# Down projection by block products: residual tiles made by GpSimd in the places of the first token sums, and added behind the sixth and the seventh product

## The chip, the core and the metric

The kernel runs on one core of a Trainium2 chip. The metric is the device time of one execution in microseconds; lower is better. The core has five engines that work side by side, each through its own queue in order: PE (TensorE, matmuls), DVE (VectorE), ACT (ScalarE), POOL (GpSimd) and SP (SyncE, which here only issues DMAs). Semaphores hold an instruction until what it needs is there, and whatever stands behind it on its engine waits as well.

## The reference, cut to what matters

One layer of an encoder with 1024 tokens of width 1024: a token mixer, cross-attention and a gated ConvFFN, each followed by a LayerNorm over the scaled input plus the result. The change lies in the last of them:

```python
h = layer_norm(DN_ALPHA * h + conv_ffn(h, w_up, b_up, w_dw, b_dw, w_down, b_down), ln3_w, ln3_b)
# conv_ffn ends in
y = jax.nn.gelu(g, approximate=False) * u        # 1024 tokens x 2816
return y @ w_down + b_down                       # 2816 x 1024
```

So the output is LayerNorm(y @ w_down + r), where r = DN_ALPHA * h + b_down is called the residual here.

## The kernel before

Everything runs in fp16 pairs: a number is split into a high and a low half (`split16`, lines 203 to 205: ACT writes the high half, DVE the low half in line 205), and each product takes three matmuls (`mm3`, lines 225 to 227).

The 2816 rows of `w_down` are 22 chunks of 128. The first 16 are multiplied by blocks in a scheme with seven products instead of eight, on sums and differences of the blocks. A product (`dprod`, line 1830) is 96 matmuls of 128x512 into four banks of PSUM. `X4` names the four banks of the products 1, 4 and 6, `W4` those of 5 and 7, `Z4` those of 2 and 3. The token sums come from `a_sums` (line 1794) and lie in four tiles made by `s_home`: X1l and X2l for the products 4 and 5, Yl and X2h for 6 and 7. In the trace they are called SX1l, SX2l, SYl and SX2h. The products 4 to 7 run with `outer=True`: the eight row blocks are the outer loop, the four banks the inner one, so the fifth product is done with SX1l in its first half and with SX2l in its second.

`into` (line 1941) brings banks to the eight result tiles `C[0]` to `C[7]` (128 tokens x 1024 each; in the trace D, and for the last two junk and unitA), by DVE in line 1945 (add or subtract) or by ACT in line 1947 (copy). The sixth product goes from X4 to both halves of C[4] to C[7] (lines 2009 and 2010), the seventh from W4 to the second halves of C[0] to C[3] (line 2012).

The residual of tile `tt` is made by `rest` (line 1997): a DMA of 512 KB from `h2_d` (line 2000), times `rw` (2001), plus `rb` (2002), and then added to C[tt] (2003). The first six are made by GpSimd in the two `wraw` buffers, the last two by DVE in a raw buffer of which there are three (`raw8`: two of the name two, one of the name ur). The same three raw buffers take the loads of the y pairs (`y_pair`, line 1839) and of the weight pairs (`w_pair`, line 1847), 1 MB each, which are split for the plain product.

The plain product (lines 2019 to 2032) covers the last six chunks. Per tile, in `order` [4, 5, 6, 7, 0, 1, 2, 3], and per half of the columns, 18 matmuls go into a bank `dn`; DVE scales it and adds it to C[tt] (line 2028, the eviction). Then `ln_tile` normalizes: DVE statistics (lines 240 to 244), a small GpSimd power (245), DVE (254), ACT (255), DVE (258) and a GpSimd addition of the bias (259); the last tile takes a shorter way (251, 252). SP stores the tile. The eight banks that `dn` takes in turn are those of X4 first (four banks), then those of W4.

The order in which each engine, SP's DMA queue among them, gets its instructions isn't written out: a planner walks through a timeline of its own and, whenever an engine is free in it, takes the earliest instruction of the program that would be ready. On the chip this order stands. Where several instructions touch one tile, they keep the order of the program.

Of the kernel before, what the change touches and what calls it, by code (L numbers as in the profile page):

```python
# [8 lines left out]
F32 = mybir.dt.float32  # L9
# [5 lines left out]
OP = mybir.AluOpType  # L15
PSUM = bass.MemoryType.PSUM

D = 1024
# [7 lines left out]
WP = 1088  # L26
# [30 lines left out]
def encoder(ctx, tc, I, out):  # L57
    nc = tc.nc
    V, A, G, T, S = nc.vector, nc.scalar, nc.gpsimd, nc.tensor, nc.sync
    anchor = [None]  # L60

    def bcast_row(ap, n, off=0):
        return bass.AP(tensor=ap.tensor, offset=ap.offset + off, ap=[[0, 128], [1, n]])
# [4 lines left out]
    wp = ctx.enter_context(tc.tile_pool(name="weights", bufs=1, reuse_waits="tile"))  # L68
    xp = ctx.enter_context(tc.tile_pool(name="acts", bufs=1, reuse_waits="tile"))
# [9 lines left out]
    def bank(name):  # L79
        key = "mem" if name == "tk" else name  # L80
        turn[key] = turn.get(key, -1) + 1
        tag = SET[name][turn[key] % len(SET[name])]
        return pp.tile([128, 512], F32, name=name, tag=tag, bufs=NB[tag])
# [29 lines left out]
    def vec(i, name):  # L113
        t = vecs.tile([128, D], F32, name=f"vec{i}", tag=f"vec{i}")
        S.dma_start(t, bcast_row(I[name], D))
        return t
# [107 lines left out]
    def mm3(ps, lh, ll, rh, rl, first, last, skip=False):  # L224
        T.matmul(ps, lh, rh, start=first, stop=False, skip_group_check=skip)  # L225
        T.matmul(ps, lh, rl, start=False, stop=False, skip_group_check=skip)  # L226
        return T.matmul(ps, ll, rh, start=False, stop=last, skip_group_check=skip)  # L227
# [1049 lines left out]
    with ExitStack() as cb_:  # L1277
# [41 lines left out]
        def raw8(shape=[128, 2 * D]):  # L1319
            i = raws[0] % 3  # L1320
            raws[0] += 1
            return rt2.tile(shape, F32, name=f"two{i}") if i < 2 else pools["ur"].tile(shape, F32, name="ur")
# [16 lines left out]
        with ExitStack() as cB:  # L1339
            lw, lb = vec(0, "ln1_w"), vec(1, "ln1_b")  # L1340
# [48 lines left out]
        def to_B1(r, tt):  # L1389

            o = slice(tt // 2 * 128, tt // 2 * 128 + 128)
            pts = []
            for q in range(2):
                pt = tbank()
                for k in range(4):
                    T.transpose(pt[:, k, :], r[:, (4 * q + k) * 128:(4 * q + k + 1) * 128], ident)
                pts.append(pt)
            B1 = B1s[:, tt // 2]
            spare = lambda i: vecs.tile([128, D], F32, name=f"spare{i}", tag=f"vec{i}")
            if tt % 2:  # L1400
                if tt == todo[-1]:
                    r = spare(1)
                dst = [r[:, i * 512:i * 512 + 512].rearrange("p (k t) -> p k t", k=4) for i in range(2)]
            else:
                dst = [B1[:, q] for q in range(2)]
            for q in range(2):
                for k in range(4):
                    i = 4 * q + k
                    evict_wb(q, dst[q][:, k], pts[q][:, k], wb2, i)
            if tt % 2 == 0:  # L1410
                for q in range(2):
                    A.activation(Bh[:, 0, q, :, o], B1[:, q], AF.Copy)
                    V.tensor_tensor(Bh[:, 1, q, :, o], B1[:, q], Bh[:, 0, q, :, o], OP.subtract)
                return
            return dst
# [246 lines left out]
        tt = rq[0][1]  # L1662
        t = to_B1(*rq.pop(0))
# [27 lines left out]
        with ExitStack() as cE:  # L1691
# [36 lines left out]
            def take(v, what):  # L1728
                bg, bu, Cg, Cu = first_half(v)
                (g0, g1), (u0, u1) = ([C[:, 1:SEQ + 1].rearrange("p (j a t) -> p a j t", a=2, t=128)[:, a]  # L1730
                                       for a in range(2)] for C in (Cg, Cu))
                j4 = lambda t: t.rearrange("p (j t) -> p j t", t=128)
                c = units.s[v][1]
                if what == "m1":
                    return A.activation(g0, j4(X[v]), AF.Identity, scale=c, bias=bg)
                elif what == "C11":
                    V.scalar_tensor_tensor(g0, j4(Z[v]), c, g0, op0=OP.mult, op1=OP.add)
                elif what == "u2":
                    return A.activation(g1, j4(X[v]), AF.Identity, scale=c, bias=bg)
                elif what == "u3":  # L1740
                    A.activation(u1, j4(X[v]), AF.Identity, scale=c, bias=bu)
                elif what == "C22":
                    V.scalar_tensor_tensor(u1, j4(W[v]), c, u1, op0=OP.mult, op1=OP.add)
                elif what == "C21":
                    A.activation(u0, j4(X[v]), AF.Identity, scale=c, bias=bu)
                elif what == "C12":
                    V.scalar_tensor_tensor(g1, j4(W[v]), c, g1, op0=OP.mult, op1=OP.add)  # L1747
# [82 lines left out]
            def dprod(banks, a, b, first, js=range(4), outer=False):  # L1830
                for j, i in [(j, i) for i in range(8) for j in js] if outer else [(j, i) for j in js for i in range(8)]:
                    t = slice(j * 128, j * 128 + 128)
                    h, l = a[i]
                    mm3(banks[j], h[:, t], l[:, t], *BF_[b][i], first and i == 0, i == 7, skip=True)
# [9 lines left out]
            def w_pair(i, h, l):  # L1844

                raw = raw8()
                S.dma_start(raw, I["w_dr"][i])
                split16(h, l, raw, sd)
                for n in range(2):
                    wl[NG + 2 * i + n] = tuple(t[:, n * 1024:n * 1024 + 1024] for t in (h, l))  # L1850
# [8 lines left out]
            for v in range(NFF):  # L1859
# [6 lines left out]
                if v > 1:  # L1866
                    first = take(v, "m1")
# [12 lines left out]
                second = take(v, "u2")  # L1880
# [55 lines left out]
        with ExitStack() as cF:  # L1936
            wk = cF.enter_context(tc.tile_pool(name="wkF", bufs=1, reuse_waits="tile"))
            C = [wk.tile([128, D], F32, name=f"D{i}") for i in range(6)]
            C += [junk.bitcast(F32), kept["A"][:, :2 * D].bitcast(F32)]

            def into(banks, a, c, how):
                for j in range(4):
                    t = C[4 * a + j][:, c * 512:c * 512 + 512]
                    if how in (OP.add, OP.subtract):
                        V.tensor_tensor(t, t, banks[j], how)
                    else:
                        A.activation(t, banks[j], AF.Copy, scale=how)
# [36 lines left out]
            rw, rb, bd = vec(0, "ln2_w"), vec(1, "ln2_b"), vec(2, "b_down")  # L1984
# [9 lines left out]
            y_pair(NG + 4, sy[1][1], *(t.rearrange("p (f t) -> p f t", f=2) for t in W5))  # L1994
            order = [4, 5, 6, 7, 0, 1, 2, 3]

            def rest(n, eng, r):

                tt = order[n]
                S.dma_start(r, h2_d[tt * 128:(tt + 1) * 128, :])  # L2000
                eng.tensor_tensor(r, r, rw, OP.mult)  # L2001
                eng.tensor_tensor(r, r, rb, OP.add)
                eng.tensor_tensor(C[tt], C[tt], r, OP.add)

            for n in range(6):
                rest(n, G, wp.tile([128, WP], F32, name="wraw", tag="wraw", bufs=2)[:, :D])
            for m in range(2):
                w_pair(m, *YH[m])
            into(X4, 1, 0, OP.add)
            into(X4, 1, 1, OP.subtract)  # L2010
            dprod(W4, n4, "B22", False, outer=True)
            into(W4, 0, 1, OP.add)
            w_pair(2, *H1[0])
            two_r, lb = raw8(), raw8()[:, :D]
            S.dma_start(lb, bcast_row(I["ln3_b"], D))
            for n in range(6, 8):
                rest(n, V, two_r[:, n % 2 * D:n % 2 * D + D])

            for tt in order:
                r = C[tt]  # L2020
                last = tt == order[-1]
                for a, n in ((0, 512), (512, 256), (768, 256)) if last else ((0, 512), (512, 512)):
                    p = bank("dn")[:, :n]
# [6 lines left out]
                for i in range(2 if last else 1):  # L2030
                    c = slice(i * 512, i * 512 + 512) if last else slice(0, D)
# [90 lines left out]
```

## Time and profile before

| | us |
|---|---|
| median of 3 runs | 1458.49 (1458.29 to 1461.16) |
| the profiled execution | 1463.53 |
| its span | 1461.7 |
| PE busy | 1417.5 (97%) |
| DVE busy | 1108.8 (76%) |
| ACT busy | 852.6 (58%) |
| POOL busy | 661.3 (45%) |

The busy times are sums over the whole span, in which the engines work side by side. What an edit near the end is worth is read from that stretch alone: in rows of a window, a timeline or the waits, whose times count from the start of the span. A row of a timeline gives the start, the duration, the engine, the line, what it writes and reads, and in brackets how long the engine was idle before and what ended that. PEclk is the clock that was granted to TensorE, as a share of full speed. Rows with a count (x2) merge instructions that follow each other.

### The profile page before, as it was taken

To read this page: it belongs to the slowest core of one execution; us is meant where nothing else is said; L and a number is where in the kernel's file an instruction comes from. 1 tells how busy PE (TensorE), PEld (TensorE's weight loads), DVE (VectorE), ACT (ScalarE), POOL (GpSimd) and SP (SyncE) were. 2 spreads that over 40 slices of the span, in tenths; PEclk is the share of its full clock that TensorE was granted. 3 is DMA by queue.
4 is the path that set the end of the run, shared out by engine and by line. 5 is a ranking of instruction groups with operands and counts; after the bars stand their busy time and mean duration, and the time that the engine had idled before them with its cause. 6 is when DMAs were issued, how large, how long until landed. Compare 5 with 4: busy or idle time off the path is not lost. (4 is left out here: it accounts for less than half of the span.)

```text
span 1461.7 us, 21452 instructions
## 1 busy us (share of the span) xinstructions
PE 1417.5 (97%) x7864; PEld 834.8 (57%) x7864; DVE 1108.8 (76%) x1986; ACT 852.6 (58%) x1399; POOL 661.3 (45%) x522
## 2 busy tenths in 40 slices
PE   8999899999999999999999999999999999999797
PEld 6999777456766777674444444444444444444344
DVE  7877866635677787679657778888888878989775
ACT  5765464664554476614446667888777858645111
POOL 4452347502232866235304154487778830004943
PEclk9999999999999999999999999999999999999999
DMA  8855654324554634653442423335444357998302
GB/s 304 306 199 177 187 184 158 113 51 113 148 158 137 222 126 142 217 179 100 106 110 85 136 87 115 118 119 189 155 151 162 137 181 231 322 321 307 136 36 87
DMA packets 133298, 237.98 MB, mean 163 GB/s; under 512 B 41284, under 2 KB 84548, under 8 KB 129479
## 3 DMA queue, kind: packets, MB, share of 16 engines
q1 hardware_dynamic: 130592, 227.44, 46.9%
q0 software_dynamic: 2448, 8.88, 1.6%
q8 instruction: 62, 1.02, 0.3%
q14 instruction: 46, 0.37, 0.1%
q10 hardware_dynamic: 150, 0.27, 0.1%
HBM read 175.12 MB, written 53.54 MB: 156 GB/s over the span
## 5 line engine op out<-in xcount | busy, mean ns | idle before, releaser
L1710 DVE SCALAR_TENSOR_TENSOR cbuf<-C,wdw,cbuf 128x1024 f32<-128x1024 f32 x44 | 69.9, 1590 | 34.6 <-ACT cbuf L1709 34.6
L227 PEld LDWEIGHTS <-wlo 128*128 128x128 f16 x574 | 56.2, 98 | 61.3 <-DVE wlo L205 2.2
L225 PEld LDWEIGHTS <-whi 128*128 128x128 f16 x574 | 56.3, 98 | 60.0 <-issue 3.5
L226 PEld LDWEIGHTS <-whi 128*128 128x128 f16 x574 | 56.3, 98 | 58.4 <-issue 1.9
L2001 POOL TENSOR_TENSOR wraw<-wraw,vec 128x1024 f32<-128x1024 f32 x6 | 17.1, 2850 | 156.8 <-DMA wraw<-h 156.8
L245 POOL TENSOR_TENSOR lnrs<-lnrs,mhalf 128x1 f32<-128x1 f32 x32 | 23.4, 732 | 137.1 <-DVE lnrs L244 130.2
L1711 DVE SCALAR_TENSOR_TENSOR cbuf<-C,wdw,cbuf 128x1024 f32<-128x1024 f32 x44 | 75.6, 1721 | 1.1
L205 DVE SCALAR_TENSOR_TENSOR wlo<-wraw,us,whi 128x1024 f16<-128x1024 f32 (+1 forms) x48 | 62.1, 1314 | 18.5 <-ACT whi L204 18.5
L1709 ACT ACTIVATE cbuf<-C,bdw,wdw 128x1024 f32<-128x1024 f32 x44 | 54.4, 1238 | 19.2 <-DVE C L1747 18.5
L204 ACT ACTIVATE whi<-wraw,us 128x1024 f16<-128x1024 f32 (+1 forms) x48 | 51.0, 1103 | 15.8 <-DVE us L177 15.3
L1568 POOL TENSOR_TENSOR wraw<-two 128x512 f32<-128x512 f32 x15 | 30.5, 2031 | 64.6 <-issue 39.1
L225 PE MATMUL tk<-whi,Bo 128*128 128x256 f16 (+1 forms) x192 | 53.7, 280 | 1.6 <-DVE stage L205 1.6
L227 PE MATMUL tk<-whi,Bo 128*128 128x256 f16 (+1 forms) x192 | 53.7, 280 | 0.0
L226 PE MATMUL tk<-wlo,Bo 128*128 128x256 f16 (+1 forms) x192 | 53.7, 280 | 0.0
L226 PE MATMUL tk<-wlo,Be 128*128 128x256 f16 (+1 forms) x192 | 52.4, 274 | 0.8 <-DVE wlo L205 0.8
L225 PE MATMUL tk<-whi,Be 128*128 128x256 f16 (+1 forms) x192 | 52.6, 274 | 0.5 <-DVE stage L205 0.5
L227 PE MATMUL tk<-whi,Be 128*128 128x256 f16 (+1 forms) x192 | 52.5, 274 | 0.0
L225 PE MATMUL S<-kq,h1T 128*128 128x512 f16 x128 | 48.5, 379 | 0.0
L226 PE MATMUL S<-kq,h1T 128*128 128x512 f16 x128 | 48.5, 379 | 0.0
L227 PE MATMUL S<-kq,h1T 128*128 128x512 f16 x128 | 48.5, 379 | 0.0
L922 POOL TENSOR_SCALAR_AFFINE_SELECT whi<-whi 128x512 f32<-128x512 f32 x16 | 10.1, 634 | 82.9 <-ACT whi L919 79.6
L1238 ACT ACTIVATE P<-P,mn 128x256 f32<-128x256 f32 (+1 forms) x64 | 35.6, 557 | 17.4 <-DVE mn L1236 16.4
(675 smaller groups left out, 5172.1 us busy)
## 6 DMA issues: line engine op xcount, KB each, us to landing
two<-in_w_up_dram SPq DMA_DIRECT2D x15, 1024.0 KB
two<-y SPq DMA_DIRECT2D x24, 512.0 KB
y<-cbuf SPq DMA_DIRECT2D x22, 512.0 KB
sv<-in_w_dn_dram SPq DMA_DIRECT2D x16, 512.0 KB
td<-sv POOLq DMA_DIRECT2D x16, 512.0 KB, 2.9
ur<-in_w_up_dram SPq DMA_DIRECT2D x7, 1024.0 KB
two<-y SPq DMA_DIRECT2D x6, 1024.0 KB
wraw<-in_w_tok_dram SPq DMA_DIRECT2D x10, 512.0 KB
```

The costliest lines, as they stand in the source:

```text
L204: A.activation(hi, src, AF.Copy, scale=s)
L205: return V.scalar_tensor_tensor(lo, src, s, hi, op0=OP.mult, op1=OP.subtract)
L225: T.matmul(ps, lh, rh, start=first, stop=False, skip_group_check=skip)
L226: T.matmul(ps, lh, rl, start=False, stop=False, skip_group_check=skip)
L227: return T.matmul(ps, ll, rh, start=False, stop=last, skip_group_check=skip)
L245: G.tensor_tensor(rs[:, 0:1], rs[:, 0:1], mhalf[:, 0:1], OP.pow)
L1238: A.activation(P[:, :nk], P[:, :nk], AF.Exp, scale=-1.0, bias=mn[:, 0:1], accum_out=mn[:, 1:2])
L1568: G.tensor_tensor(S1, A21, A22, OP.add)
L1709: A.activation(c, C[:, 1:SEQ + 1], AF.Identity, scale=wdw[:, 1, j:j + 1], bias=bdw[:, j:j + 1])
L1710: V.scalar_tensor_tensor(c, C[:, 0:SEQ], wdw[:, 0, j:j + 1], c, op0=OP.mult, op1=OP.add)
L1711: V.scalar_tensor_tensor(c, C[:, 2:SEQ + 2], wdw[:, 2, j:j + 1], c, op0=OP.mult, op1=OP.add)
L2001: eng.tensor_tensor(r, r, rw, OP.mult)
```

## The change

All eight residuals are now made by GpSimd, in two tiles `R` of 128 x 4096 that take the places of the token sums X1l and X2l. Making a residual (load, product, sum) and adding it to its C tile are two steps now. The first four additions stand behind X4's additions of the sixth product in the program, on GpSimd; the last four behind W4's additions of the seventh, two on GpSimd and two on DVE. The raw buffer in which DVE made its two residuals is no longer taken.

```diff
+            R = [xp.tile([128, 4096], F32, name="R" + t, tag=t).rearrange("p (i c) -> p i c", i=4) for t in ("X1l", "X2l")]
+
+            def rest(n):
+
+                r, tt = R[n // 4][:, n % 4], order[n]
                 S.dma_start(r, h2_d[tt * 128:(tt + 1) * 128, :])
-                eng.tensor_tensor(r, r, rw, OP.mult)
-                eng.tensor_tensor(r, r, rb, OP.add)
-                eng.tensor_tensor(C[tt], C[tt], r, OP.add)
-
-            for n in range(6):
-                rest(n, G, wp.tile([128, WP], F32, name="wraw", tag="wraw", bufs=2)[:, :D])
+                G.tensor_tensor(r, r, rw, OP.mult)
+                G.tensor_tensor(r, r, rb, OP.add)
+                return C[tt], r
+
+            first = [rest(n) for n in range(4)]
             for m in range(2):
                 w_pair(m, *YH[m])
             into(X4, 1, 0, OP.add)
             into(X4, 1, 1, OP.subtract)
+            for c, r in first:
+                G.tensor_tensor(c, c, r, OP.add)
+            second = [rest(n) for n in range(4, 8)]
             dprod(W4, n4, "B22", False, outer=True)
             into(W4, 0, 1, OP.add)
             w_pair(2, *H1[0])
-            two_r, lb = raw8(), raw8()[:, :D]
+            lb = raw8()[:, :D]
             S.dma_start(lb, bcast_row(I["ln3_b"], D))
-            for n in range(6, 8):
-                rest(n, V, two_r[:, n % 2 * D:n % 2 * D + D])
+            for n, (c, r) in enumerate(second):
+                (G if n < 2 else V).tensor_tensor(c, c, r, OP.add)
```

More of the change, by code (lines that the diff above doesn't have):

```diff
@@ L1995, in encoder @@
             order = [4, 5, 6, 7, 0, 1, 2, 3]
-            def rest(n, eng, r):
-                tt = order[n]
+            R = [xp.tile([128, 4096], F32, name="R" + t, tag=t).rearrange("p (i c) -> p i c", i=4) for t in ("X1l", "X2l")]
+            def rest(n):
+                r, tt = R[n // 4][:, n % 4], order[n]
                 S.dma_start(r, h2_d[tt * 128:(tt + 1) * 128, :])
-                eng.tensor_tensor(r, r, rw, OP.mult)
-                eng.tensor_tensor(r, r, rb, OP.add)
-                eng.tensor_tensor(C[tt], C[tt], r, OP.add)
-            for n in range(6):
-                rest(n, G, wp.tile([128, WP], F32, name="wraw", tag="wraw", bufs=2)[:, :D])
+                G.tensor_tensor(r, r, rw, OP.mult)
+                G.tensor_tensor(r, r, rb, OP.add)
+                return C[tt], r
+            first = [rest(n) for n in range(4)]
             for m in range(2):
```

## The prediction

> **What bounds the kernel now.** I read the windows view over the end of the span first (columns: stretch, length, then busy time and count for each engine, the granted TensorE clock, the DMA share and GB/s).
>
> ```profile
> 1317.60:1338.30 20.70, 20.70 (x98) 9.37 (x97) 18.25 (x19) 11.14 (x11) 2.82 (x1) 1.00 0.94 347
> 1359.10:1379.87 20.77, 20.77 (x97) 9.17 (x94) 12.39 (x4) 2.00 (x1) 18.98 (x8) 1.00 0.41 152
> 1379.87:1389.33 9.46, 0.01 (x2) 0.01 (x1) 9.46 (x6) 0.00 (x0) 7.04 (x2) 0.75 0.33 108
> 1389.33:1394.50 5.17, 5.17 (x13) 1.86 (x14) 3.53 (x6) 0.00 (x0) 4.18 (x2) 0.50 0.01 6
> 1402.00:1454.50 52.50, 52.41 (x261) 25.31 (x259) 35.87 (x64) 8.69 (x7) 19.97 (x14) 1.00 0.15 61
> 1454.50:1461.70 7.20, 0.00 (x0) 0.00 (x0) 3.98 (x8) 0.00 (x0) 1.25 (x2) 0.86 0.38 146
> ```
>
> PE is full through the fifth block product (first row) and the seventh (second row, to 1379.87), then idle for 9.46 us, then at a granted clock of 0.50, and full again to 1454.5; a tail of 7.2 us without matmuls ends the span. So PE sets the pace, and the one hole in it is just where the edit lies. The waits and PE's timeline say who made the hole:
>
> ```profile
> PE dn L225 <- DVE D L1945: 9.5, 1, 9.5
> 1379.49 0.38 PE L227 MATMUL zw<-whi,SX2h 128*128 128x512 f16 x1
> 1389.33 0.61 PE L225 MATMUL dn<-BY,yq 128*128 128x512 f16 x1 [9.46 <-DVE D L1945]
> 1394.85 0.38 PE L226 MATMUL dn<-wlo,whi 128*128 128x512 f16 x1
> 1454.13 0.27 PE L227 MATMUL dn<-whi,wlo 128*128 128x256 f16 x1
> ```
>
> The plain product's first bank is one of X4's, and X4 is released by the additions of line 1945. They ran this late because of DVE's and POOL's (GpSimd's) queues; these are rows of their timelines (start, duration, instruction):
>
> ```profile
> 1353.35 4.45 DVE L205 SCALAR_TENSOR_TENSOR BY<-two,sc,BY 128x2048 f16<-128x2048 f32 x1
> 1367.48 2.03 DVE L2001 TENSOR_TENSOR two<-two,vec 128x1024 f32<-128x1024 f32 x1 [9.69 <-DMA two<-h]
> 1380.37 4.42 DVE L205 SCALAR_TENSOR_TENSOR BY<-ur,sc,BY 128x2048 f16<-128x2048 f32 x1
> 1384.72 3.36 DVE L2002 TENSOR_TENSOR two<-two,vec 128x1024 f32<-128x1024 f32 x1
> 1388.00 2.47 DVE L1945 TENSOR_TENSOR D<-D,dx 128x512 f32<-128x512 f32 x4
> 1335.48 7.07 POOL L2001 TENSOR_TENSOR wraw<-wraw,vec 128x1024 f32<-128x1024 f32 x2 [151.72 <-DMA wraw<-h]
> 1376.04 3.33 POOL L2003 TENSOR_TENSOR unitA<-unitA,wraw 128x1024 f32<-128x1024 f32 x1
> 1397.37 2.35 POOL L2003 TENSOR_TENSOR D<-D,wraw 128x1024 f32<-128x1024 f32 x1
> ```
>
> X4's last matmul is a whole product earlier than 1379.87 (the second row's 20.77 us), near 1359.1, yet its additions start at 1388.00. Two things stand ahead of them. The additions read what POOL wrote into the same C tiles (the last of these four, unitA, ends at 1379.37). And DVE itself idles 9.69 us for the residual rows that it makes, and then has them and two weight splits in front. Those rows and the third weight pair were late because of SP's queue:
>
> ```profile
> 1327.14 1.51 SPq L2000 DMA_DIRECT2D wraw<-h  x2
> 1344.72 4.72 SPq L1847 DMA_DIRECT2D two<-in_w_dr_dram  x2
> 1355.67 4.68 SPq L2000 DMA_DIRECT2D wraw<-h  x2
> 1360.45 0.37 SPq L1847 DMA_DIRECT2D ur<-in_w_dr_dram  x1
> ```
>
> The rows wait at SP's head for a wraw buffer that POOL still adds from, and the weights stand behind them.
>
> **The change part by part.** *The hole.* X4's additions no longer follow POOL's: the order on each C tile is now addition first, residual after. DVE loses four products and sums and their wait for DMA. With no hole, the matmul due after 1379.49 comes one warm step later, at 1379.71 (the 20.77 us for 96 matmuls of the seventh product make 0.216 us a step). That regains 1389.33 − 1379.71 = 9.62 us. From 1389.33 to 1394.85 lie 13 steps, 5.52 us against 2.81 warm: another 2.71 us. Together 12.3 us: PE would end near 1441.9, and with the same tail the span would be 1449.4.
>
> Cover for this: two more things must be there by 1379.7. First, X4's additions. DVE has from about 1341 six splits of line 205 (three y pairs, three weight pairs), four of which end at 1357.8 today.
>
> ```profile
> 1330.75 2.35 DVE L205 SCALAR_TENSOR_TENSOR wlo<-two,sc,whi 128x2048 f16<-128x2048 f32 x1
> 1336.95 3.37 DVE L205 SCALAR_TENSOR_TENSOR SX2h<-wlo,sc,SX2h 128x1024 f16<-128x1024 f32 x1
> 1344.61 4.45 DVE L205 SCALAR_TENSOR_TENSOR wlo<-two,sc,whi 128x2048 f16<-128x2048 f32 x1
> 1342.50 8.78 POOL L2002 TENSOR_TENSOR wraw<-wraw,vec 128x1024 f32<-128x1024 f32 x2
> 1390.32 2.36 POOL L2001 TENSOR_TENSOR wraw<-wraw,vec 128x1024 f32<-128x1024 f32 x1 [3.33 <-DMA wraw<-h]
> 1390.39 1.27 DVE L1945 TENSOR_TENSOR junk<-junk,dx 128x512 f32<-128x512 f32 x2
> ```
>
> A split takes 2.35 us with POOL idle and 4.45 beside it; a POOL operation 2.36 alone and 4.39 beside splits. An addition from PSUM (0.63) and a POOL operation (2.36) leave each other alone. The edit loads four residual tiles, not two, ahead of the y pairs: 1 MB more, 3.0 us at the 347 GB/s of the fifth product's row, so I let the splits start at 1344. Six at 4.45 end at 1370.7, eight additions at 0.62 at 1375.7: 4.0 us to spare. Second, the last weight pair: its SP entry no longer stands behind a residual load, so its split, today at 1380.37, is among those six.
>
> *POOL.* It loses no operation and gains four: 16 products and sums into R, four additions behind X4, two behind W4, 22 for 18. When can it start? R takes the places of SX1l and SX2l.
>
> ```profile
> L227 PE MATMUL zw<-BY,SX1l x16: 379/379/380, 1318.0 to 1327.7; 128*128 128x512 f16 x16
> L227 PE MATMUL zw<-BY,SX2l x16: 379/379/380, 1328.3 to 1338.1; 128*128 128x512 f16 x16
> ```
>
> The fifth product goes through its tiles in order, so the first half of R is free at 1328.0, 0.9 us behind today's first load, and the second at 1338.5. DMA is full there (share 0.94), so the first tile should land about a microsecond behind today's 1335.48: 1336.5. From there nothing waits for buffers. By 1336.5 plus 20 operations all eight residuals are made and four added. Alone that is 20 × 2.35 = 47.0 us. Beside splits it is more: each costs POOL 4.39 − 2.35 = 2.04 us, and six and a half of them are left: 13.3 us. Sum 60.3, a mean of 3.01, end 1396.8. The same count on today's trace: 18 × 2.35 = 42.3, and 20.3 us of DVE work with two SBUF inputs (the six splits, half a split, four residual operations) at 2.04 per 2.35, makes 59.9; the 18 operations took
>
> ```profile
> L2001 POOL TENSOR_TENSOR wraw<-wraw,vec x6: 2342/2658/3759, 1335.5 to 1390.3; 128x1024 f32<-128x1024 f32 x6
> L2002 POOL TENSOR_TENSOR wraw<-wraw,vec x6: 2355/3801/4411, 1342.5 to 1394.9; 128x1024 f32<-128x1024 f32 x6
> L2003 POOL TENSOR_TENSOR D<-D,wraw x4: 2346/3372/4409, 1351.2 to 1397.4; 128x1024 f32<-128x1024 f32 x4
> ```
>
> from 1335.5 to 1399.7, 64.2 us with some 5 us of waits for DMA. So the count holds. The bounds for 20 operations are 47.0 us (none beside a split) and 87.8 (all at 4.39): end 1383.5 or 1424.3. I take 1396.8, since DVE has only that much to collide with.
>
> *DVE's queue behind it.* The last two residuals are added by DVE, and an instruction that waits holds up all behind it, the evictions of the plain product above all.
>
> ```profile
> 1401.55 2.35 DVE L2003 TENSOR_TENSOR D<-D,two 128x1024 f32<-128x1024 f32 x2
> 1403.82 0.75 DVE L2028 SCALAR_TENSOR_TENSOR D<-dn,sc,D 128x512 f32<-128x512 f32 x1
> 1407.97 0.74 DVE L2028 SCALAR_TENSOR_TENSOR D<-dn,sc,D 128x512 f32<-128x512 f32 x1
> 1413.85 0.74 DVE L2028 SCALAR_TENSOR_TENSOR junk<-dn,sc,junk 128x512 f32<-128x512 f32 x1
> ```
>
> Today these two additions stand just ahead of the first eviction, and I expect the same. So the first eviction comes at 1396.8 + 1.2 = 1398.0, although its bank is full at 1379.7 + 18 × 0.216 = 1383.6. Is that late? In the catch-up the rows of line 2028 show tiles at +4.15 and then every 5.88 us, while PE needs 36 × 0.216 = 7.77 a tile. The eighth tile would be evicted 39.4 us after the first, at 1437.4; its bank is full at 1383.6 + 54.4 = 1438.0. So DVE catches up by the last tile as long as the first eviction starts by 1398.6, and every microsecond beyond is lost. PE has eight banks, four tiles, and doesn't stop for the evictions before 1379.7 + 31.1 = 1410.8. POOL's two additions behind W4 (4.7 us, to 1401.5) delay the first normalization's small POOL step by 0.4 us (due 3.1 us behind the eviction, 1401.1). With 1398.0 + 0.4 so close to 1398.6 and about 3 us of doubt either way, I charge 0.8 us.
>
> *Sum.* −9.6 − 2.7 + 0.8 = −11.5 us. The profiled execution took 1463.5 us (span 1461.7 and 1.8 around it), so it would be 1452.0; the median of the runs shown, 1458.5, is 5.0 us below the profiled one, and I move it by the same amount: 1447.0.
>
> **Rules against it.** The trace prices one sum of 1024 columns at 1.18 us on DVE (2.35 for two, above) and 2.35 on POOL, so the edit buys DVE's freedom with twice the time. The Trainium skill (GPSIMD Engine Reference, section Engine selection) advises the vector engine for elementwise work, GpSimd being about twice as slow; that is the third rival below. A hole shorter than today's may be cheaper than in proportion: the only one at this place is 9.6 us long and cost 2.7 us of clock. The Trainium skill (TensorE: Matmul & The Clock Gate, section on oscillation) puts the limit for a loss of clock at gaps of about 3.4 us; by it a hole of 3 us would cost 3 us and not 5.7, which no run here shows.
>
> **The rivals.** *A smaller hole remains* (0.13): the 4.0 us to spare before X4's banks are used up, by y pairs landing later than 1344 or by the splits being queued otherwise. Additions 3 us late leave a hole of 3 and up to 2.7 of clock: −11.5 + 5.7 = −5.8, 1452.7. For it: DMA share 0.94 when R loads; against: it falls to 0.41 in the seventh product.
>
> *The residual loads are late* (0.12): SP places R behind the y pairs' third load, which waits for a raw buffer until about 1337, when DVE begins the split of 1336.95. Then POOL starts near 1344, the first eviction comes at 1405.5, 6.9 us beyond the limit: 1449.4 + 6.9 = 1456.3 of span, −5.4, 1453.1.
>
> *POOL becomes the pace, and the kernel slower* (0.08): all its operations collide, and DVE stands at its two additions meanwhile. The price is first eviction minus 1398.6. It eats the whole gain at 1410.9, where PE also runs out of banks, and costs 0.2% (2.9 us) from 1413.8, that is from a mean of (1413.8 − 1.2 − 1336.5) / 20 = 3.8 us for a POOL operation; today's mean is 3.3 with more DVE work beside it. At the upper bound, 1425.5, it loses 26.9 us and 2.7 of clock: about 1476.
>
> *It doesn't do what it says* (0.06): the planner leaves X4's additions behind something that POOL or a late load holds, as they stand behind residual operations today; the hole stays, and the time is 1458 ± 2.
>
> **How the numbers follow.** The forecast, hole gone and eviction near 1398, has 0.61, and its own range is 1446 to 1450. 0.2% (2.9 us) is about what a measurement can tell from no change. The two partial rivals lie at 1453, still faster. Faster: 0.61 + 0.13 + 0.12 = 0.86; the no-change rival and the nearer part of the third give same 0.07; slower 0.07. The range goes from the whole 12.3 us and 0.7 of spread, 1445.5, over the partial rivals to 1456.0.
>
> **What would show it.** In the changed profile: no wait of PE before the first dn matmul, at about 1379.7, clock 1.00 there; line 1945 on X4 done by 1376; POOL's first residual operation near 1336.5 and its twentieth ending near 1397 with a mean near 3.0 us; the two DVE additions last ahead of the first eviction near 1398, and the eighth tile waiting for PE again; PE's last matmul near 1441.9 and the tail unchanged. It is wrong if PE still waits at the first dn matmul, or if the evictions of the last tile come late with PE done: then POOL's time was mis-sized.

## The result and the profile after

| | before | after |
|---|---|---|
| median, us | 1458.49 (7 runs, 1457.77 to 1468.78) | 1451.78 (7 runs, 1447.84 to 1455.87) |
| ratio | | 0.9948, 95% interval 0.9925 to 0.9971 |
| profiled execution, us | 1463.53 | 1451.78 |
| its span | 1461.7 | 1450.1 |

The change makes the kernel faster: 6.7 us between the medians, where 11.5 were forecast. The two profiled executions differ by 11.8 us (spans: 11.6). So the first question is not where the change failed, but why the profiles promise more than the runs. All ratios here leave out two slow executions, one of order_alone (2965 us) and one of the kernel before beside it (4297 us).

The windows of the profile after, in the columns of the prediction's first fence (seventh product, plain product, tail):

```profile
1359.10:1380.40 21.30, 21.30 (x100) 9.64 (x99) 10.48 (x13) 0.95 (x1) 21.30 (x9) 1.00 0.00 1
1380.40:1442.70 62.30, 62.30 (x307) 29.85 (x305) 40.96 (x65) 8.68 (x7) 41.30 (x23) 1.00 0.13 52
1442.70:1450.10 7.40, 0.07 (x1) 0.00 (x0) 4.15 (x9) 0.00 (x0) 2.06 (x2) 0.78 0.37 142
```

PE goes from the seventh product into the plain one without a gap and at full clock (1.00 throughout); the tail without matmuls is about as long as before (7.4 us in this window against 7.2). The same in PE's timeline:

```profile
1380.19 0.38 PE L227 MATMUL zw<-whi,SX2h 128*128 128x512 f16 x1
1380.40 0.38 PE L225 MATMUL dn<-BY,yq 128*128 128x512 f16 x1
1442.50 0.27 PE L227 MATMUL dn<-whi,wlo 128*128 128x256 f16 x1
```

DVE's timeline shows the additions that made the hole, early now, and what takes their place as its last wait. Line 2021 adds the last two residuals; the evictions are line 2032 now.

```profile
1360.08 3.67 DVE L205 SCALAR_TENSOR_TENSOR BY<-ur,sc,BY 128x2048 f16<-128x2048 f32 x1 [0.69 <-ACT BY L204]
1363.68 2.47 DVE L1945 TENSOR_TENSOR D<-D,dx 128x512 f32<-128x512 f32 x4
1378.66 2.63 DVE L1945 TENSOR_TENSOR D<-D,zw 128x512 f32<-128x512 f32 x4 [10.12 <-PE zw L227]
1384.47 3.35 DVE L2021 TENSOR_TENSOR D<-D,RX2l 128x1024 f32<-128x1024 f32 x1 [3.18 <-POOL RX2l L2004]
1390.06 3.35 DVE L2021 TENSOR_TENSOR D<-D,RX2l 128x1024 f32<-128x1024 f32 x1 [2.24 <-POOL RX2l L2004]
1393.33 0.74 DVE L2032 SCALAR_TENSOR_TENSOR D<-dn,sc,D 128x512 f32<-128x512 f32 x1
1403.10 0.21 DVE L254 TENSOR_SCALAR lnrs<-lnmv,lnrs 128x1 f32<-128x1 f32 x1 [6.43 <-POOL lnrs L245]
1403.23 0.74 DVE L2032 SCALAR_TENSOR_TENSOR D<-dn,sc,D 128x512 f32<-128x512 f32 x1
1438.88 0.75 DVE L2032 SCALAR_TENSOR_TENSOR D<-dn,sc,D 128x512 f32<-128x512 f32 x1
```

X4's additions begin at 1363.68 instead of 1388.00. DVE then waits for PE, twice for the residuals that GpSimd makes, and for 6.43 us for the first normalization's small GpSimd step (line 245), which stands behind all of GpSimd's additions:

```profile
1339.23 6.97 POOL L2003 TENSOR_TENSOR RX1l<-RX1l,vec 128x1024 f32<-128x1024 f32 x2 [154.81 <-PE zw L227]
1395.59 2.35 POOL L2013 TENSOR_TENSOR unitA<-unitA,RX1l 128x1024 f32<-128x1024 f32 x1
1397.89 4.66 POOL L2021 TENSOR_TENSOR D<-D,RX2l 128x1024 f32<-128x1024 f32 x2
1402.51 0.56 POOL L245 TENSOR_TENSOR lnrs<-lnrs,mhalf 128x1 f32<-128x1 f32 x1
```

GpSimd works from 1339.23 to 1402.55 without a break. And SP's rows show that no load waits for GpSimd's additions any more:

```profile
1332.45 1.89 SPq L2002 DMA_DIRECT2D RX1l<-h  x4
1339.66 4.69 SPq L1847 DMA_DIRECT2D two<-in_w_dr_dram  x2
1344.40 1.85 SPq L2002 DMA_DIRECT2D RX2l<-h  x4
1350.69 0.33 SPq L1847 DMA_DIRECT2D ur<-in_w_dr_dram  x1
```

### The profile page after: what moved, and what is told of

It is laid out like the page before. It is cut to its first block, busy times and chain, and to the rows that moved or that the text cites. A ratio compares the mean times of both kernels' runs of the same rounds, so it can differ in the third digit from the quotient of the medians.

```text
span 1450.1 us, 21441 instructions
## 1 busy us (share of the span) xinstructions
PE 1413.6 (97%) x7864; PEld 833.7 (57%) x7864; DVE 1091.5 (75%) x1982; ACT 853.1 (59%) x1399; POOL 666.5 (46%) x526
## 5 line engine op out<-in xcount | busy, mean ns | idle before, releaser
L2003 POOL TENSOR_TENSOR RX1l<-RX1l,vec 128x1024 f32<-128x1024 f32 x4 | 15.8, 3957 | 154.8 <-PE zw L227 154.8
L245 POOL TENSOR_TENSOR lnrs<-lnrs,mhalf 128x1 f32<-128x1 f32 x32 | 23.4, 731 | 122.7 <-DVE lnrs L244 116.8
L205 DVE SCALAR_TENSOR_TENSOR wlo<-wraw,us,whi 128x1024 f16<-128x1024 f32 (+1 forms) x48 | 62.1, 1312 | 18.7 <-ACT whi L204 18.7
```

Of the source, the lines that this page charges most:

```text
L205: return V.scalar_tensor_tensor(lo, src, s, hi, op0=OP.mult, op1=OP.subtract)
L245: G.tensor_tensor(rs[:, 0:1], rs[:, 0:1], mhalf[:, 0:1], OP.pow)
L2003: G.tensor_tensor(r, r, rw, OP.mult)
```

## The experiments

Three theories. **A**: PE's hole and the lower clock behind it were worth 12.3 us, always; the difference between profile and runs lies elsewhere. **B**: GpSimd's queue makes the evictions late in many executions of the changed kernel, which eats part of the gain. **C**: the hole is shorter in an ordinary execution of the kernel before than in the one that was profiled.

The programs are alike up to the fifth product. Its start, read from the tile SX1l, varies all the same between executions, from 1313.0 to 1320.7 us, so I measure from it. The table holds, per profile: the start of the fifth product, the first dn matmul, the hole ahead of it, the distance from the first dn matmul to the first line 254 (the step that lets DVE go on from the first tile to the second), the span behind the start of PE's last matmul (the tail), and the span behind the fifth product's start. Ratios are to the kernel before on the same chip; where there is none, there was a single execution.

| kernel | fifth | dn | hole | to 254 | tail | fifth to end | ratio, 95% interval |
|---|---|---|---|---|---|---|---|
| before | 1317.6 | 1389.33 | 9.5 | 18.5 | 7.6 | 144.1 | |
| before_2 | 1316.2 | 1388.44 | 9.9 | 18.6 | 7.6 | 144.4 | |
| before_3 | 1317.3 | 1389.88 | 10.3 | 18.7 | 7.6 | 144.9 | |
| before_4 | 1315.1 | 1383.37 | 6.0 | 18.6 | 7.6 | 140.7 | |
| before_5 | 1316.2 | 1384.92 | 6.4 | 20.7 | 7.6 | 140.8 | |
| after | 1318.2 | 1380.40 | none | 22.7 | 7.6 | 131.9 | 0.9948, 0.9925 to 0.9971 |
| after_2 | 1315.2 | 1377.32 | none | 24.9 | 9.8 | 134.0 | 0.9947, 0.9928 to 0.9966 |
| after_3 | 1316.7 | 1378.81 | none | 25.1 | 10.0 | 134.2 | 0.9951, 0.9933 to 0.9969 |
| last_pool | 1313.0 | 1375.18 | none | 26.0 | 10.8 | 135.1 | 0.9977, 0.9961 to 0.9993 |
| first_dve | 1320.7 | 1382.90 | none | 21.6 | 7.6 | 131.9 | 0.9943, 0.9921 to 0.9964 |
| first_dve_2 | 1319.0 | 1381.16 | none | 19.0 | 7.5 | 131.8 | 0.9935, 0.9914 to 0.9957 |
| adds_dve | 1316.0 | 1378.15 | none | 20.1 | 7.5 | 131.8 | 0.9936, 0.9917 to 0.9955 |
| places_alone | 1315.5 | 1377.62 | none | 27.8 | 12.7 | 136.9 | 0.9974, 0.9959 to 0.9990 |
| order_alone | 1317.5 | 1379.69 | none | 26.3 | 11.0 | 135.3 | 0.9964, 0.9944 to 0.9985 |

**before_2 to before_5: how long is the hole?** No edit: the kernel before, four times.

> The kernel before once more, for a second look at the length of its hole. The profiled execution of before took 1463.5 us, 5.0 us above the median of its runs. Theory A (that execution differed somewhere else, the hole is always some 9.5 us and 2.7 us of clock): PE waits 9 to 10 us ahead of the first dn matmul again. Rival C (an ordinary execution has a shorter hole, so that the change has less to win back there): in an execution near 1458 us PE waits only about 4 to 6 us.

> The kernel before a third time. The starts of the fifth product differ by some 4 us either way between executions of kernels that are alike up to there, so the hole has to be read against that start: 71.7 and 72.2 us from it to the first dn matmul in the two profiles so far, 62.2 without a hole. Theory A: about 72 again in any execution. Rival C: in an execution near the median of 1457 us the distance is 66 to 68.

> The kernel before a fourth time, for the same question: about 72 us from the fifth product's start to the first dn matmul (theory A), or some of them at 66 to 68 (rival C).

> The kernel before a fifth time, for the spread of the hole: 9.5, 9.9, 10.3 and 6.0 us in four profiles. Rival C says that the hole goes with how late the first residual rows land behind the start of the fifth product (17.9, 18.1, 18.1 us for the long ones, 15.3 for the short one): whatever the time, the hole should be that distance less 8.2 to 9.3 us.

before_2 and before_3 took 1462.3 and 1464.0 us and have holes of 9.9 and 10.3. before_4 and before_5 took 1457.5 and 1458.8 us, near the medians of the kernel before on their chips (1459.0 and 1458.9), and have holes of 6.0 and 6.4, a little above the 4 to 6 us that rival C expected there. Here are rows of before_4 (GpSimd's first residual, DVE's first residual, X4's additions, PE's wait) and three windows of it (hole, matmuls at the lower clock, the rest of the plain product):

```profile
1330.37 6.71 POOL L2001 TENSOR_TENSOR wraw<-wraw,vec 128x1024 f32<-128x1024 f32 x2 [149.14 <-DMA wraw<-h]
1362.12 1.42 DVE L2001 TENSOR_TENSOR two<-two,vec 128x1024 f32<-128x1024 f32 x1 [6.48 <-DMA two<-h]
1382.05 2.47 DVE L1945 TENSOR_TENSOR D<-D,dx 128x512 f32<-128x512 f32 x4
1383.37 0.61 PE L225 MATMUL dn<-BY,yq 128*128 128x512 f16 x1 [5.99 <-DVE D L1945]
```

```profile
1377.30:1383.37 6.07, 0.08 (x1) 0.00 (x1) 6.07 (x5) 0.00 (x0) 3.74 (x1) 0.89 0.55 167
1383.37:1389.00 5.63, 5.63 (x14) 2.06 (x15) 3.53 (x6) 0.00 (x0) 4.54 (x2) 0.51 0.01 6
1389.00:1448.50 59.50, 59.48 (x294) 28.49 (x292) 38.75 (x67) 8.69 (x7) 24.68 (x17) 1.00 0.14 54
```

The chain is the same, only earlier against PE. GpSimd's first residual starts 17.9, 18.1, 18.1, 15.3 and 15.6 us behind the start of the fifth product in the five profiles, and the hole is that less 8.4, 8.2, 7.8, 9.3 and 9.2 us. So the hole goes with the landing of the first residual rows. It goes more closely still with the residual that DVE makes: that starts 49.9, 50.4, 50.8, 47.1 and 47.7 us behind the start of the fifth product, and X4's additions follow it by 19.7 to 20.5 us in all five. The clock is lost all the same: the plain product takes 64.8 us from its first matmul to its last behind the hole of 6.0 (1383.37 to 1448.20) and 62.1 in the profile after, 2.7 more, as behind the hole of 9.5; behind the hole of 6.4 it is 2.4 more. C holds and A falls as far as its "always" goes: in the two traces near the median, hole and clock are worth 8.7 to 8.8 us, not 12.3. Five traces don't show how often either kind of hole comes.

**after_2 and after_3: does the changed kernel get it all?** No edit.

> The changed kernel once more, timed in five rounds. Theory A: no wait of PE ahead of the first dn matmul, a tail of 7.5 us behind PE's last matmul, ratio to before 0.992 (11.5 us). Rival C: the same profile, but a ratio of 0.994 to 0.996, as in the first timing. Rival B (GpSimd's queue often makes the last evictions late): the last matmul ends over 1 us ahead of the last eviction's start, and the tail behind PE is longer than 7.5 us in slower executions.

> The changed kernel a third time, beside two that relieve GpSimd. In five kernels without a hole so far, the tail behind PE's last matmul was 7.6 us as long as the second tile's DVE step behind the first normalization (line 254) came within 22.7 us of the first dn matmul, and longer by each microsecond beyond. If this is the rule, the tail here is 7.6 plus what that distance exceeds 22.7 by; the changed kernel's two traces have 22.7 and 24.9. Ratio to before 0.994 to 0.996.

PE never waits, but the tail is 9.8 and 10.0 us. The ratios, 0.9947 and 0.9951, are those of rival C and not A's 0.992. after_3's line 254, its last evictions and PE's end:

```profile
1403.91 0.21 DVE L254 TENSOR_SCALAR lnrs<-lnmv,lnrs 128x1 f32<-128x1 f32 x1 [6.44 <-POOL lnrs L245]
1439.62 0.74 DVE L2032 SCALAR_TENSOR_TENSOR D<-dn,sc,D 128x512 f32<-128x512 f32 x1
1440.91 0.27 PE L227 MATMUL dn<-whi,wlo 128*128 128x256 f16 x1
1443.66 0.47 DVE L2032 SCALAR_TENSOR_TENSOR D<-dn,sc,D 128x256 f32<-128x256 f32 x1
```

The last eviction starts 2.7 us behind the start of PE's last matmul; in the profile after it is 0.3 (1442.83 against 1442.50). The expected rule holds: 25.1 − 22.7 = 2.4, 7.6 + 2.4 = 10.0. So B is right too, for two of the three traces of the changed kernel.

What differs between the three is when GpSimd begins. These are its first operations in after_2 and after_3:

```profile
1338.28 6.98 POOL L2003 TENSOR_TENSOR RX1l<-RX1l,vec 128x1024 f32<-128x1024 f32 x2 [156.92 <-DMA RX1l<-h]
1340.01 6.97 POOL L2003 TENSOR_TENSOR RX1l<-RX1l,vec 128x1024 f32<-128x1024 f32 x2 [157.13 <-DMA RX1l<-h]
```

That is 23.1 and 23.4 us behind the start of the fifth product, against 21.0 in the profile after, and in all three line 254 comes 63.9 us later. So the start of GpSimd's first residual, which went with the hole before, goes with the tail now.

**last_pool: two operations more for GpSimd.**

```diff
-                (G if n < 2 else V).tensor_tensor(c, c, r, OP.add)
+                G.tensor_tensor(c, c, r, OP.add)
```

> The changed kernel with the last two residuals added by GpSimd too, so that GpSimd has 24 operations instead of 22 and DVE none of them. GpSimd as the pace (my third rival, and the 0.8 us that I charged): the small GpSimd step of the first normalization comes two operations later less what DVE no longer disturbs, some 4 us, behind 1402.5; the first eviction comes earlier, at about 1384, but the second at about 1407 instead of 1403.2; as the changed kernel's eighth tile is just caught up, the end moves out by 3 to 4 us against it, so a ratio to before of about 0.997. If GpSimd's queue isn't the pace, the time is that of the changed kernel.

```profile
1391.31 9.26 POOL L2021 TENSOR_TENSOR D<-D,RX2l 128x1024 f32<-128x1024 f32 x4
1382.15 0.75 DVE L2032 SCALAR_TENSOR_TENSOR D<-dn,sc,D 128x512 f32<-128x512 f32 x1 [6.07 <-POOL D L2013]
1401.13 0.21 DVE L254 TENSOR_SCALAR lnrs<-lnmv,lnrs 128x1 f32<-128x1 f32 x1 [15.63 <-POOL lnrs L245]
```

Measured from the first dn matmul, the first eviction comes 6.0 us earlier than in the profile after (7.0 instead of 12.9), and it doesn't help: DVE then stands 15.63 us at line 254. From GpSimd's first operation to line 254 it is 66.6 us (1334.58 to 1401.13) against 63.9, 2.7 more, not 4. The ratio is 0.9977, as expected, though its interval still overlaps that of after_2 on the same chip. The traced execution was the fastest of twelve, 4.9 us below their median, so the traces don't show all that the ordinary ones lose. GpSimd's queue is what the evictions wait for here, and the step that counts is line 254, not the first eviction.

**first_dve, first_dve_2, adds_dve: four and six operations less for GpSimd.** In first_dve and first_dve_2 the first four additions go to DVE, which waits there for the seventh product; in adds_dve all eight do.

```diff
             for c, r in first:
-                G.tensor_tensor(c, c, r, OP.add)
+                V.tensor_tensor(c, c, r, OP.add)
```

> The changed kernel with the first four residuals added by DVE, which waits 10 us for the seventh product there. DVE's four additions run from about 1368.5 to 1382, beside GpSimd; GpSimd has 18 operations and is free for the first normalization near 1397 instead of 1402.5, so the second eviction comes near 1398 instead of 1403. Theory A (PE sets the end, evictions are caught up anyway): the same time as the changed kernel within 1 us. Rival B (late evictions cost the ordinary runs of the changed kernel): 2 to 4 us faster than it, ratio to before 0.992.

> The changed kernel with the first four residuals added by DVE, again: distance 21 to 22 us, tail 7.6, PE sets the end. If ordinary executions of the changed kernel lose 1 to 2 us by late evictions, this one is faster by as much: ratio to before 0.993 to 0.995. If they lose nothing: the same ratio as the changed kernel.

> The changed kernel with all eight residuals added by DVE, GpSimd making them only (16 operations). GpSimd is done with them near 1389 and free for the first normalization whenever DVE gets there: distance 17 to 20 us, tail 7.6. Since the evictions are caught up either way, the same time as with four on DVE, within 1 us; faster only if these still lost something.

Rows of adds_dve: the first two additions on DVE beside GpSimd, then line 254, and the eighth tile waiting for PE again:

```profile
1367.85 6.51 DVE L2013 TENSOR_TENSOR D<-D,RX1l 128x1024 f32<-128x1024 f32 x2
1398.21 0.21 DVE L254 TENSOR_SCALAR lnrs<-lnmv,lnrs 128x1 f32<-128x1 f32 x1 [0.67 <-POOL lnrs L245]
1436.63 0.75 DVE L2032 SCALAR_TENSOR_TENSOR D<-dn,sc,D 128x512 f32<-128x512 f32 x1 [0.97 <-PE dn L227]
```

An addition takes 3.3 us on DVE here, beside GpSimd, and costs nothing at the end, since DVE was idle. All three have a tail of 7.5 or 7.6 us and 131.8 or 131.9 us from the fifth product to the end. first_dve has this although GpSimd begins 24.0 us behind the start of the fifth product, later than in all three traces of the changed kernel. So these three traces lose nothing to evictions. The runs don't show a gain over the changed kernel. first_dve's median is 1450.59 us against 1450.57 for after_2 on the same chip, where rival B expected 2 to 4 us. On another chip first_dve_2 and adds_dve have 1449.5 and 1449.1 us against 1450.9 for after_3; their ratios, 0.9935 and 0.9936 against 0.9951, lie within its interval.

**places_alone: the new places without the new order.** The first four are added where they were, in `rest`, ahead of X4's additions.

```diff
                 G.tensor_tensor(r, r, rb, OP.add)
+                if n < 4:
+                    G.tensor_tensor(C[tt], C[tt], r, OP.add)
                 return C[tt], r
...
-            for c, r in first:
-                G.tensor_tensor(c, c, r, OP.add)
```

> The changed kernel, but the first four residuals are added to their C tiles at the old place in the program, ahead of X4's additions, so that these wait for GpSimd again. The first theory says that X4's additions come late because they stand behind GpSimd's: then a hole returns ahead of the first or the third dn bank. The rival: what made them late was DVE's own residuals and the loads held back at the head of SP's queue, which the new places alone remove. By the changed kernel's trace GpSimd would add to C[4] at about 1364 and to C[7] at 1386, while PE needs these banks from 1380 and from 1392: no hole, and the time of the changed kernel within 1.5 us. I expect the rival to hold.

```profile
1380.85 1.28 DVE L1945 TENSOR_TENSOR junk<-junk,dx 128x512 f32<-128x512 f32 x2 [7.95 <-POOL junk L2006]
1385.46 1.28 DVE L1945 TENSOR_TENSOR unitA<-unitA,dx 128x512 f32<-128x512 f32 x2 [3.33 <-POOL unitA L2006]
1392.40 9.09 DVE L2021 TENSOR_TENSOR D<-D,RX2l 128x1024 f32<-128x1024 f32 x2 [3.27 <-POOL RX2l L2004]
1405.43 0.21 DVE L254 TENSOR_SCALAR lnrs<-lnmv,lnrs 128x1 f32<-128x1 f32 x1 [0.67 <-POOL lnrs L245]
```

No hole, as expected, although X4's additions wait for GpSimd again, the last until 1385.46: the banks are still in time for PE. So of the two things that the prediction found ahead of X4's additions, GpSimd's additions alone don't make the hole. But the trace isn't the changed kernel's: it has 5.1 us of tail more than 7.6. With the additions ahead, GpSimd makes the last four sums at its end, DVE's two additions wait for them until 1392.40 and then run beside GpSimd (9.09 us for two), and line 254 comes at 27.8. I had looked at the hole alone.

**order_alone: the new order without the new places.** The two wraw buffers and DVE's raw buffer stay.

```diff
-            for n in range(6):
-                rest(n, G, wp.tile([128, WP], F32, name="wraw", tag="wraw", bufs=2)[:, :D])
...
+            pairs = two_raws(0)
             for m in range(2):
                 w_pair(m, *YH[m])
             into(X4, 1, 0, OP.add)
             into(X4, 1, 1, OP.subtract)
+            add_on(pairs, G)
+            add_on(two_raws(2), G)
+            pairs = two_raws(4)
...
+            add_on(pairs, G)
...
             for n in range(6, 8):
-                rest(n, V, two_r[:, n % 2 * D:n % 2 * D + D])
+                add_on([rest(n, V, two_r[:, n % 2 * D:n % 2 * D + D])], V)
```

Here `two_raws` makes two residuals in the wraw buffers and `add_on` adds them.

> The kernel before with the new order alone: the first four residuals are added behind X4's additions, but all stay in the old places (two buffers for GpSimd, a raw buffer for DVE's two). The hole should be gone or under 3 us, since X4's additions wait for splits and DVE's residuals only. But GpSimd has to wait for X4's additions with both its buffers full, and then makes the other four residuals with a wait for DMA each pair: 14 operations of 2.35 to 3 us and two waits of some 4 us from about 1377, to 1418 or later, and the first normalization's small GpSimd step stands behind them. First theory (PE's hole is all): as fast as the changed kernel. GpSimd as the pace: the evictions come 15 us later than in the changed kernel and the end 10 to 15 us later, near before or slower.

```profile
1351.34 0.33 SPq L1847 DMA_DIRECT2D ur<-in_w_dr_dram  x1
1367.00 2.47 DVE L1945 TENSOR_TENSOR D<-D,dx 128x512 f32<-128x512 f32 x4
1368.42 4.67 POOL L2010 TENSOR_TENSOR D<-D,wraw 128x1024 f32<-128x1024 f32 x2 [21.52 <-DVE D L1945]
1370.81 19.88 SPq L2000 DMA_DIRECT2D wraw<-h  x4
1391.53 4.71 POOL L2001 TENSOR_TENSOR wraw<-wraw,vec 128x1024 f32<-128x1024 f32 x2 [1.19 <-DMA wraw<-h]
1406.01 0.21 DVE L254 TENSOR_SCALAR lnrs<-lnmv,lnrs 128x1 f32<-128x1 f32 x1 [13.63 <-POOL lnrs L245]
```

No hole either. GpSimd stands 21.52 us with both buffers full and is done at 1405.4, 13 us earlier than I expected, since it starts again at 1368.4 instead of 1377 and works beside a DVE that is mostly idle. The price is 3.4 us of tail, not 10 to 15.

Either half of the change closes the hole alone, then. They share one thing: the third weight pair's load no longer stands behind residual loads in SP's queue. It goes out at 1351.34 here and at 1349.40 in places_alone, against 1360.45 before; here GpSimd's later four residual loads, two of which stood just ahead of it, come at 1370.81 and after. No run changes SP's queue alone, so that this is enough isn't shown. Both halves together bring line 254 1 to 5 us earlier than either alone, by the traces (22.7 to 25.1 us against 27.8 and 26.3). The ratios of the two, 0.9974 and 0.9964, lie above the changed kernel's 0.9947 to 0.9951, but the intervals overlap.

## Why the prediction was right, and which terms were off

**The hole and the clock**: right, for the two executions compared. PE's wait is gone, the first dn matmul follows the seventh product by one step, the clock stays at 1.00, and the plain product takes 62.1 us. From the fifth product to the end it is 131.9 us instead of 144.1: 12.2 us, forecast 12.3. The first of the two reasons given for the hole, GpSimd's additions ahead of X4's, was not needed for it (places_alone).

**The cover of X4's additions**: right, with more to spare than worked out. They end at 1368.5, 11.9 us ahead of the first dn matmul, where I had 4.0: I had put R's loads ahead of all y pairs, but two of the three went first (SP's row of R at 1332.45 shows the place), so that the splits began at 1337 and not at 1344.

**GpSimd's count**: the start was 2.7 us later than the 1336.5 that I took, mostly for the same reason, so a part of my rival of late loads came true (it had 7.5 us). The mean of the twenty operations is (1397.94 − 1339.23) / 20 = 2.94 us against 3.01. The twentieth ends at 1397.9, forecast 1396.8.

**The first eviction**: 1393.3, forecast 1398.0. GpSimd finished the eighth residual ahead of three of its additions. What I had as a small addition to it, 0.4 us of wait for the first normalization's GpSimd step, was 6.43 us and is what counts. The two errors cancel, which is partly luck: 1398.0 + 0.4 and the 4.0 us from the first eviction to line 254 in the trace of before (1403.82 to 1407.84) make 1402.4, 22.7 us behind the forecast 1379.7, as measured.

```profile
1407.84 0.21 DVE L254 TENSOR_SCALAR lnrs<-lnmv,lnrs 128x1 f32<-128x1 f32 x1 [0.67 <-POOL lnrs L245]
```

The limit itself was right in size. A first eviction by 1398.6 means a line 254 22.9 us behind the first dn matmul; the nine traces without a hole give 22.7, with about a microsecond of tail for each one beyond (2.2, 2.4, 3.2, 3.4 and 5.1 us of tail for 2.2, 2.4, 3.3, 3.6 and 5.1). In the profile after, the eighth tile is just caught up: its last eviction starts as PE's last matmul ends, where I expected it to wait for PE.

**The 0.8 us charged for it**: 0.0 in the profile after, 2.2 and 2.4 in the two others, 1.5 in the mean.

**The step that was off most** is the last of the sum, where the 5.0 us between the profiled execution and the median are taken off both kernels alike. That took the profiled hole for the hole of every run. Most of the 5.0 us was the hole itself: it was 3.1 to 3.5 us longer in the profiled execution than in the two traces near the median. With those two traces and the three of the changed kernel, 6.2 of hole, 2.6 of clock and 1.5 of late evictions give −7.3; the three pairs of medians say −6.7, −6.3 and −8.0. So the mechanism held, and two sizes were off: the hole was 6.2 and not 9.6, and the charge for GpSimd 1.5 and not 0.8. With so few traces the sum is a rough one. The measured 1451.8 lies in the whole range but outside the forecast's own, 1446 to 1450: the whole range was wide enough because of rivals that did not come true as they were told.

**The rival with GpSimd as the pace** was half true: it decides the end in two of the changed kernel's three traces, through line 254 and not the first eviction, at a microsecond for each one beyond the limit, but never comes near the point where it would eat the gain. The Trainium skill (GPSIMD Engine Reference, section Engine selection) speaks for the vector engine in elementwise work; the additions moved back to DVE agree with it as far as the traces go (a tail of 7.5 or 7.6 in all three, instead of 7.6, 9.8 and 10.0).

**Open** stays why the residual rows land 15.3 us behind the start of the fifth product in one execution and 18.1 in another, and why that product itself starts anywhere from 1313.0 to 1320.7. A part of the first is there already when SP sends the loads: 9.6, 9.6, 9.8, 8.1 and 8.4 us behind the start of the fifth product in the five traces of before, and 14.2, 16.1 and 16.3 in the three of the changed kernel. No run here varied that.

## What to carry to other kernels

A stall in one profiled execution is one sample: if that execution is slower than the median, its stall may be what makes it so, and the gain is better priced from several executions. When a hole on the busiest engine is closed, work out which engine is next to be late and from which step; here one small operation at the end of a helper's queue set it, not the first visible wait. And a load that waits for its buffer at the head of a DMA queue holds up the loads behind it, which have nothing to do with that buffer.

## What the runs showed of the hardware

Holes of 6.0, 6.4 and 9.5 us cost about the same in clock: 2.7, 2.4 and 2.7 us, 12 to 14 matmuls at a granted clock near 0.5 (0.51, 0.52 and 0.50). The Trainium skill (TensorE: Matmul & The Clock Gate, section on oscillation) gives a limit of some 3.4 us of idle time for this; all holes here lie above it, so they agree with it and don't test it.

The same sum on DVE with both inputs in SBUF (line 2002, 128x1024) took 1.22 us with GpSimd idle (order_alone) and 3.36 to 3.37 us beside GpSimd's operations (before).
